# Transformer block on one core: adaLN column sums on VectorE alone, the modulated copy of x on ScalarE, and the residual gate's columns summed in the key projections

## The chip, the cores and the metric

The kernel runs on one core of a Trainium2 chip. The metric is the device time of one execution in microseconds (us), lower is better. The kernel before takes 989.82 us, the median of three runs (989.09 to 990.09).

The names of the engines in the profile: PE is TensorE (matrix products and transposes), DVE is VectorE, ACT is ScalarE, POOL is GpSimd, SP is SyncE, which here issues the transfers. Each engine runs its own instructions strictly in order and waits on semaphores for the others.

## The reference, cut to what matters

One block of a streaming encoder on x of 1024 tokens by 1024 channels, all in float32:

```
shift, scale, gate = split(c @ w_ada + b_ada, 3)
h = rms_norm(x, norm_w) * (1 + scale) + shift
cq, ckv, k_rope, gate_a, q_b, k_b, v_b, f_b, gate_b, mg_a, mg_b = split(h @ w_in)
q  = rms_norm(cq)  @ w_uq          # branch A, 8 heads
kv = rms_norm(ckv) @ w_ukv
o_a = attention_a(norm(q), norm(k), v)        # chunk-causal mask
o_b = attention_b(norm(q_b), norm(k_b), v_b)  # forget gates, causal
merged = sigmoid(mg_a) * ((o_a * silu(gate_a)) @ w_branch_a)
       + sigmoid(mg_b) * ((o_b * silu(gate_b)) @ w_branch_b)
out = x + gate * (merged @ w_out)
```

shift and scale are needed before the first product of h. gate, the residual gate, is needed only in the last line.

## The kernel before, in words

**Precision.** Every product is done in three passes: an operand is split into a high part (a cast to fp32r) and a low part (the rest), and hi·hi, hi·lo and lo·hi are added. So each operand costs a cast, mostly on ScalarE, and a subtraction, mostly on VectorE.

**Order of work.** Nothing schedules the program: each engine's instructions stand in the order in which the Python code emits them. SyncE issues the transfers in the same way, one queue, in order.

**Stage 1** (`phase0`, 0 to about 87 us). x is loaded, normed, transposed and kept as xT, 8 blocks (kt) of 128 channels on the partitions by 1024 tokens. The columns of shift and scale for a block come from two tiles of w_ada (128x1024): each is multiplied by c, spread over all partitions (`cb`), and summed along the row. `ada_cols(kt, e)` does that for tile e (0 is shift, 1 is scale): engine "d" is one VectorE instruction (L339), "p" is the product on GpSimd (L342), and "a" the sum on ScalarE after it (L344). `gain(kt)` makes the factor and the addend of a block, gs (two VectorE instructions, L348 and L349). `high(kt)` writes hT_hi = xT·gs + gs on ScalarE (L355), `modulate(kt)` the same in full precision over xT on VectorE (L359), and `low(kt)` hT_lo = xT - hT_hi on VectorE (L365). Then `products(kt)` adds a block into the q latents: 8 token tiles x 3 passes = 24 matmuls of 424 columns for each block; the last pass reads hT_lo. Blocks 0 and 1 are handled piece by piece as x arrives (token tiles 0 to 5 first, "last" are tiles 6 and 7), blocks 2 to 7 in the loop `for kt in range(2, KT)`, where an iteration makes the gain and the high part of block kt + 1 and the low part of block kt.

**The residual gate before.** In the same loop the 8 tiles of w_gate are loaded (`gate_load`) and summed with c (`gate_sum`): half by GpSimd (L932) and ScalarE (L936), half by VectorE (L939), the last of them in the next stage, `latents`. There the bias is added to the 8 columns, gcol. `gate_row` turns gcol into a row and stores it: a transpose on TensorE (pgT), a scaled copy on VectorE (grow, L949), a transfer to gate_d (L950). It is called in the q projections, after the third pair of token tiles.

**Stage 2** (`g2k`, about 220 to 275 us) is the key and value projection of branch A, two token tiles in each of four calls (sp): kv matmuls, ScalarE copies, the low part of v on VectorE (L831), square sums (L834), rsqrt, the scaled k (L841), and stores to va_d and ka_d one call later (L807). Between and behind the calls `fill_to` puts matmuls that are only due later: here branch B's q, k and v (PSUM tile b, 48 matmuls of 256 columns for each, copied out by ScalarE and VectorE, L883, and stored to vb_d, L918). Two PSUM banks take turns for them. After stage 2 the heads' operands are loaded back (qs from qa_d, L1087, then v, q and ks from ka_d) and the attention starts.

Of the kernel before, what the change touches and what calls it, by code (L numbers as in the profile page):

```python
# [10 lines left out]
F32 = mybir.dt.float32  # L11
# [30 lines left out]
class Slots:  # L42
    """Equal pieces of SBUF, taken and given back by hand; the one given back longest ago goes first."""
# [31 lines left out]
class Net:  # L75
# [162 lines left out]
    # ------------------------------------------------------------ phase 0  # L238
    def phase0(self):
# [46 lines left out]
        def warm(n, src):  # L286
            """Keeps the tensor engine's clock up while it waits for x."""
# [23 lines left out]
        def broadcast_c():  # L311
            """c along the free dimension of every partition, through a diagonal and a product with ones."""
# [15 lines left out]
        def ada_rows(kt, bank):  # L328
            """The shift of a block whose rows lie on the partitions."""
# [6 lines left out]
        def ada_cols(kt, e, engine="d"):  # L336
            w, a = wada[kt][e], acc[:, kt, e:e + 1]
            if engine == "d":
                nc.vector.scalar_tensor_tensor(out=w, in0=w, scalar=1.0, in1=self.cb, op0=ALU.mult, op1=ALU.mult,  # L339
                                               accum_out=a)  # L340
            elif engine == "p":
                nc.gpsimd.tensor_tensor(out=w, in0=w, in1=self.cb, op=ALU.mult)  # L342
            else:
                nc.scalar.activation(w, w, AF.Copy, accum_out=a)  # L344
# [12 lines left out]
        def modulate(kt, sts=range(ST), engine="d"):  # L357
            c = slice(sts[0] * P, (sts[-1] + 1) * P)
            (nc.vector if engine == "d" else nc.gpsimd).tensor_scalar(  # L359
                out=xT[:, kt, c], in0=xT[:, kt, c], scalar1=gs[:, kt, 1:2], scalar2=gs[:, kt, 0:1],  # L360
                op0=ALU.mult, op1=ALU.add)
# [15 lines left out]

        def modulated(kt, sts):
            high(kt, sts)
            modulate(kt, sts)  # L380
            low(kt, sts)
# [67 lines left out]
        ada_cols(2, 0, "p")  # L449
# [3 lines left out]
        high(1, most)  # L453
        banks[4], banks[5] = self.bank("o", "cq_o"), self.bank("f", "cq_f")
        products(0, (4, 5), (0, 1))
        modulate(1, most)
# [7 lines left out]
        ada_cols(2, 0, "a")  # L464
# [4 lines left out]
        load_cq(2)  # L469
        ada_cols(2, 1)  # L470
# [6 lines left out]
        ada_cols(3, 0, "p")  # L477
        load(5)
        for kt in range(2):
            high(kt, last)  # L480
        high(2)
        for kt in range(2):
            modulate(kt, last)
            low(kt, last)
        for kt in range(2):
            products(kt, last)
        ada_cols(4, 0, "p")
        load_cq(3)
        load(6)
        for kt in range(2, KT):  # L490
            if 2 < kt < KT - 2:
                ada_cols(kt + 2, 0, "p")
            if kt + 1 < KT:
                ada_cols(kt + 1, 0, "a")
# [3 lines left out]
            modulate(kt)  # L498
            low(kt)
# [6 lines left out]
            if kt == 5:  # L506
                self.gate_load((0, 1))
                self.gate_sum((0, 1), "p")
            if kt == 6:
                self.gate_load((2, 3))  # L510
                self.gate_sum((0, 1), "a")
                self.gate_sum((2, 3), "p")
            if kt == 7:
                self.gate_load((4, 5))
# [8 lines left out]
    # ------------------------------------------------------------ latents  # L523
# [33 lines left out]
    def latents(self):  # L557
# [43 lines left out]
        self.gate_load((6, 7))  # L601
        self.gate_sum((2,), "a")
        self.gate_sum((4,))
# [7 lines left out]
        self.gate_sum((5, 6, 7))  # L611
# [9 lines left out]
        self.gate_sum((3,), "a")  # L621
# [30 lines left out]
        nc.vector.tensor_tensor(out=self.gcol, in0=self.gcol, in1=self.b_gate, op=ALU.add)  # L652
# [82 lines left out]
    # ------------------------------------------------------------ branch A operands  # L735
# [62 lines left out]
    def store(self, *items):  # L798
        """(dst, src, slot): put on the queue one unit later, when the data is there, so that no load waits behind it.
        A function among them makes more of these when its turn comes."""  # L800
# [44 lines left out]
    # ------------------------------------------------------------ work off the critical path  # L845
    def g1b(self, hook):
        """q, k and v of branch B: 256 columns at a time, two token tiles in a bank."""
# [78 lines left out]
    def gate_sum(self, chs, engine="d"):  # L926
        """128 columns of the adaLN gate each."""
        nc = self.nc
        for ch in chs:
            if engine == "p":  # L930
                w = self.wg[ch]
                nc.gpsimd.tensor_tensor(out=w, in0=w, in1=self.cb, op=ALU.mult)  # L932
                continue
            w = self.wg.pop(ch)
            if engine == "a":
                nc.scalar.activation(w, w, AF.Copy, accum_out=self.gcol[:, ch:ch + 1])  # L936
                self.U.put(w)
                continue
# [4 lines left out]
    def gate_row(self):  # L943
        """The gate as a row, quartered (the two factors of a half that the merge gates leave out)."""
        nc = self.nc
        pg = self.bank("t", "pgT")
# [10 lines left out]
    def fillers(self):  # L957
        """All GEMMs that only have to be done in time, some matmuls at a time; True where an accumulation ends."""
# [172 lines left out]
    def prep_b(self, n):  # L1131
        """The same for heads n and n + 1 of branch B, turned together: rows 0-63 of a transpose are head n's."""
# [16 lines left out]
        def group(nm, src, vec, g):  # L1149
# [41 lines left out]
    def scores(self, n, i):  # L1191
        """Scores of q tile i of head n and their maximum; the rest of the softmax is returned."""
# [35 lines left out]
    def turn(self, n, g, j):  # L1228
        """Transposes k block j of P for q tiles 4g..4g+3; the products with V are returned."""
# [114 lines left out]
    # ------------------------------------------------------------ all  # L1344
# [189 lines left out]
```

## Time and profile before

| | |
|---|---|
| median of three runs | 989.82 us (989.09 to 990.09) |
| profiled execution, span from its first to its last instruction | 989.3 us |
| mean granted clock of TensorE | 0.990 |
| PE busy | 954.5 us, 96% |
| DVE busy | 659.8 us, 67% |
| ACT busy | 475.7 us, 48% |
| POOL busy | 250.8 us, 25% |

The profiled execution has no time of its own in the results; its span is what the trace covers. TensorE is busy nearly everywhere, so the time is the sum of TensorE's work and of the stretches in which it waits. On the page's picture of 40 slices such stretches are in the first four (PE 6, 4, 7, 9 tenths) and in the last one. The granted clock is 1.0 at TensorE's higher level (2.4 GHz) and 0.5 at the lower one (1.2 GHz).

### The profile page before, as it was taken

The numbers are of one execution on the slowest core, as the hardware profiler recorded it, in microseconds if no ns is written. First come the engines' busy times: TensorE is split into PE (matmuls) and PEld (weight loads), VectorE is DVE, ScalarE is ACT, GpSimd is POOL, SyncE is SP. The second block draws the span as 40 slices with busy tenths as digits, with TensorE's granted clock in tenths as the row PEclk, the third lists the DMA queues.
The fourth block names the chain that finished last, engine by engine and source line by source line (L and its number), as shares of the span: only waits on it lengthen the run. The fifth ranks groups of instructions, "written<-read, shape, count | busy, mean of one in ns | idle before, by whom it ended". The sixth has DMA issues, their size and how long they took to land.

```text
span 989.3 us, 15335 instructions
## 1 busy us (share of the span) xinstructions
PE 954.5 (96%) x5550; PEld 833.1 (84%) x5550; DVE 659.8 (67%) x1399; ACT 475.7 (48%) x962; POOL 250.8 (25%) x279
## 2 busy tenths in 40 slices
PE   6479999999999999999999999999999999999998
PEld 6379999999998888888888888888888888887887
DVE  6997787676734766757667667677676767495222
ACT  6347653344334655655646566566565644143000
POOL 4843222220001222221223233333332220045000
PEclk9889999999999999999999999999999999999999
DMA  9733113346485223424224232231321554643321
GB/s 345 285 128 131 52 55 107 124 150 221 155 251 149 67 95 84 139 66 109 84 65 119 77 108 66 86 109 65 118 87 45 181 181 148 228 148 126 100 92 64
DMA packets 80700, 123.95 MB, mean 125 GB/s; under 512 B 5896, under 2 KB 47504, under 8 KB 80624
## 3 DMA queue, kind: packets, MB, share of 16 engines
q1 hardware_dynamic: 80624, 122.96, 38.1%
q8 instruction: 44, 0.72, 0.3%
q14 instruction: 32, 0.26, 0.1%
HBM read 87.29 MB, written 35.66 MB: 124 GB/s over the span
## 4 chain that ended last, share of the span: by engine, by line
PE 85%; DVE 8%; DMA 4%; issue 1%; ACT 1%; SPq 0%; POOL 0%; ACTq 0%; DVEq 0%; POOLq 0%
PE f L127 31%; PE b L127 12%; PE out L127 9%; PE s L127 8%; PE o L127 7%; PE pt L136 6%; PE q L127 3%; PE ckv L127 2%; PE kv L127 2%; DVE hT_lo L1046 1%; DVE hT_lo L365 1%; DMA ks_u<-ka_d 1%; DVE wada_u L339 1%; PE cq_s L127 1%; DVE xT L359 1%
## 5 line engine op out<-in xcount | busy, mean ns | idle before, releaser
L1240 ACT CAST pp_u<-pt 128x512 fp32r<-128x512 f32 x192 | 92.1, 480 | 181.6 <-PE pt L136 167.8
L1241 DVE TENSOR_TENSOR pp_u<-pt,pp_u 128x512 fp32r<-128x512 f32 x192 | 106.6, 556 | 79.2 <-ACT pp_u L1240 77.1
L127 PE MATMUL f<-hT_hi,hi_f_u 128*128 128x512 f32 x384 | 153.6, 400 | 0.0
L127 PE MATMUL f<-hT_hi,lo_f_u 128*128 128x512 f32 x384 | 153.4, 400 | 0.0
L127 PE MATMUL f<-hT_lo,hi_f_u 128*128 128x512 f32 x384 | 153.2, 399 | 0.0
L127 PE MATMUL s<-k_u,q_u 96*128 96x512 f32 (+6 forms) x480 | 116.4, 361 | 0.7 <-ACT p_h L1220 0.7
L127 PE MATMUL b<-hi_b_u,hT_hi 128*128 128x256 f32 x384 | 109.6, 285 | 0.0
L127 PE MATMUL b<-hi_b_u,hT_lo 128*128 128x256 f32 x384 | 108.6, 283 | 0.0
L127 PE MATMUL b<-lo_b_u,hT_hi 128*128 128x256 f32 x384 | 108.6, 283 | 0.0
L1224 POOL TENSOR_SCALAR p_u<-p_u,rs 128x640 f32<-128x640 f32 (+1 forms) x64 | 65.2, 1018 | 164.4 <-DVE rs L1223 95.9
L1224 POOL TENSOR_SCALAR p_h<-p_h,rs 128x128 f32<-128x128 f32 (+1 forms) x64 | 38.6, 603 | 245.5 <-DVE rs L1223 205.7
L1214 DVE TENSOR_REDUCE nm<-s 128x1 f32<-128x128 f32 (+7 forms) x128 | 97.0, 758 | 4.4
L127 PE MATMUL o<-pp_u,v_u 128*128 128x512 f32 (+7 forms) x384 | 94.2, 340 | 0.0
L127 PEld LDWEIGHTS f<-hT_hi,lo_f_u 128*128 128x128 f32 x384 | 72.4, 189 | 11.9
L127 PEld LDWEIGHTS f<-hT_lo,hi_f_u 128*128 128x128 f32 x384 | 72.5, 189 | 11.2
L127 PEld LDWEIGHTS f<-hT_hi,hi_f_u 128*128 128x128 f32 x384 | 72.5, 189 | 11.1
L127 PEld LDWEIGHTS s<-k_u,q_u 96*128 96x128 f32 (+2 forms) x480 | 76.7, 190 | 6.1 <-ACT p_h L1220 1.2
L127 PEld LDWEIGHTS o<-pp_u,v_u 128*128 128x128 f32 (+1 forms) x384 | 61.8, 161 | 19.6
L127 PEld LDWEIGHTS b<-lo_b_u,hT_hi 128*128 128x128 f32 x384 | 73.6, 192 | 0.3
L127 PEld LDWEIGHTS b<-hi_b_u,hT_hi 128*128 128x128 f32 x384 | 73.6, 192 | 0.3
L127 PEld LDWEIGHTS b<-hi_b_u,hT_lo 128*128 128x128 f32 x384 | 73.6, 192 | 0.0
L136 PEld LDWEIGHTS pt<-ident,p_u 128*128 128x128 f32 x416 | 52.7, 140 | 16.6
(319 smaller groups left out, 2072.0 us busy)
## 6 DMA issues: line engine op xcount, KB each, us to landing
raw_f_u<-in_w_t SPq DMA_DIRECT2D x24, 512.0 KB
wada_u<-in_w_ada SPq DMA_DIRECT2D x16, 512.0 KB
mg_d<-th_h SPq DMA_DIRECT2D x32, 256.0 KB
mg_h<-mg_d SPq DMA_DIRECT2D x32, 256.0 KB
raw_b_u<-in_w_b SPq DMA_DIRECT2D x12, 512.0 KB
x_u<-in_x SPq DMA_DIRECT2D x8, 512.0 KB
raw_wg_u<-in_w_gate SPq DMA_DIRECT2D x8, 512.0 KB
va_d<-vhl_u SPq DMA_DIRECT2D x8, 512.0 KB
```

The source lines that it names most:

```text
L127: self.nc.tensor.matmul(out, lhsT=l, rhs=r, start=start, stop=stop)
L136: self.nc.tensor.transpose(out=out, in_=in_, identity=self.ident)
L339: nc.vector.scalar_tensor_tensor(out=w, in0=w, scalar=1.0, in1=self.cb, op0=ALU.mult, op1=ALU.mult, accum_out=a)
L359: (nc.vector if engine == "d" else nc.gpsimd).tensor_scalar(out=xT[:, kt, c], in0=xT[:, kt, c], scalar1=gs[:, kt, 1:2], scalar2=gs[:, kt, ...
L365: nc.vector.tensor_tensor(out=lo[:, kt, c], in0=xT[:, kt, c], in1=hi[:, kt, c].bitcast(F32), op=ALU.subtract)
L1046: nc.vector.tensor_tensor(out=self.hT_lo[x], in0=mA[c1][:, x[2]], in1=self.hT_hi[x].bitcast(F32), op=ALU.subtract)
L1214: nc.vector.tensor_reduce(out=nm, in_=sv, axis=AX.X, op=ALU.max, negate=True)
L1224: nc.gpsimd.tensor_scalar(out=p[:, 0:w], in0=p[:, 0:w], scalar1=rs, scalar2=0.0, op0=ALU.mult, op1=ALU.add)
L1240: nc.scalar.copy(ph[:, c0:], pt[:, c0:])
L1241: nc.vector.tensor_tensor(out=pl[:, c0:], in0=pt[:, c0:], in1=ph[:, c0:].bitcast(F32), op=ALU.subtract)
```

## The change: what is computed where

1. Stage 1: both sums of blocks 2 to 7 are single VectorE instructions. GpSimd's products and ScalarE's sums are gone.
2. Stage 1: `modulate` of block 1 on, and of the last token tiles of block 0, is a ScalarE instruction behind `high` of the same block. In the loop, the low part of block kt now stands first in its iteration.
3. The residual gate's sums leave stage 1 and `latents`. They stand in stage 2: a new input c_row (4 KB) is spread over the partitions by one transfer (cb2, 512 KB in SBUF), two tiles of w_gate are loaded ahead of each of the four calls, and two VectorE sums stand behind each call. `gate_row`, with the bias, follows the fourth.

Other lines of the diff drop comments. `high` is as before (L349 in the changed kernel).

```
     def ada_cols(kt, e):
         w, a = wada[kt][e], acc[:, kt, e:e + 1]
-            elif engine == "p":
-                nc.gpsimd.tensor_tensor(out=w, in0=w, in1=self.cb, op=ALU.mult)
-            else:
-                nc.scalar.activation(w, w, AF.Copy, accum_out=a)
+        nc.vector.scalar_tensor_tensor(out=w, in0=w, scalar=1.0, in1=self.cb,
+            op0=ALU.mult, op1=ALU.mult, accum_out=a)
     def modulate(kt, sts=range(ST), engine="d"):
+        if engine == "a":
+            nc.scalar.activation(xT[:, kt, c], xT[:, kt, c], AF.Identity,
+                scale=gs[:, kt, 1:2], bias=gs[:, kt, 0:1])
+            return
...
         for kt in range(2):
             high(kt, last)
+            modulate(kt, last, "a")
+        for kt in range(2):
+            low(kt, last)
         high(2)
+        modulate(2, engine="a")
         for kt in range(2, KT):
-            if 2 < kt < KT - 2:
-                ada_cols(kt + 2, 0, "p")
+            low(kt)
             if kt + 1 < KT:
-                ada_cols(kt + 1, 0, "a")
+                ada_cols(kt + 1, 0)
                 ada_cols(kt + 1, 1)
                 gain(kt + 1)
                 high(kt + 1)
-            modulate(kt)
-            low(kt)
+                modulate(kt + 1, engine="a")
...
-            if kt == 5:
-                self.gate_load((0, 1))
-                self.gate_sum((0, 1), "p")
...
     def gate_row(self):
+        self.U.put(self.cb)
+        nc.vector.tensor_tensor(out=self.gcol, in0=self.gcol, in1=self.b_gate, op=ALU.add)
         pg = self.bank("t", "pgT")
         self.transpose(pg[0:8, 0:P], self.gcol)
...
                 for sp in range(4):
                     self.g2q(sp)
-                    if sp == 2:
-                        self.gate_row()
...
+                self.cb = self.U.get([P, D], F32, "cb2")
+                nc.sync.dma_start(self.cb, t["c_row"].broadcast_to([P, D]))
+                self.gate_load((0, 1))
                 for sp in range(4):
                     self.g2k(sp)
+                    self.gate_sum((2 * sp, 2 * sp + 1))
+                    if sp < 3:
+                        self.gate_load((2 * sp + 2, 2 * sp + 3))
                     self.fill_to(self.pe_time + 6500)
+                self.gate_row()
                 self.store()
```

VectorE, loop of stage 1, before. A row is the line, the operation and what it writes and reads; wada41 is the scale tile of block 4. These are the iterations for blocks 2 and 3:

```order
L339 SCALAR_TENSOR_TENSOR wada31_u20_21_344,ada_109<-wada31_u20_21_344,cb_u13_14_240 128x1024
L348 TENSOR_SCALAR gs_108<-ada_109,vec_91 128x1
L349 SCALAR_TENSOR_TENSOR gs_108<-ada_109,b1_97,vec_91 128x1
L359 TENSOR_SCALAR xT_107<-xT_107,gs_108 128x1024
L365 TENSOR_TENSOR hT_lo_81<-xT_107,hT_hi_80 128x1024
L339 SCALAR_TENSOR_TENSOR wada41_u3_25_446,ada_109<-wada41_u3_25_446,cb_u13_14_240 128x1024
L348 TENSOR_SCALAR gs_108<-ada_109,vec_91 128x1
L349 SCALAR_TENSOR_TENSOR gs_108<-ada_109,b1_97,vec_91 128x1
L359 TENSOR_SCALAR xT_107<-xT_107,gs_108 128x1024
L365 TENSOR_TENSOR hT_lo_81<-xT_107,hT_hi_80 128x1024
```

The same engine and place in the changed kernel (wada40 is the shift tile of block 4):

```order
L361 TENSOR_TENSOR hT_lo_81<-xT_107,hT_hi_80 128x1024
L338 SCALAR_TENSOR_TENSOR wada30_u19_20_343,ada_109<-wada30_u19_20_343,cb_u13_14_240 128x1024
L338 SCALAR_TENSOR_TENSOR wada31_u20_21_344,ada_109<-wada31_u20_21_344,cb_u13_14_240 128x1024
L342 TENSOR_SCALAR gs_108<-ada_109,vec_91 128x1
L343 SCALAR_TENSOR_TENSOR gs_108<-ada_109,b1_97,vec_91 128x1
L361 TENSOR_TENSOR hT_lo_81<-xT_107,hT_hi_80 128x1024
L338 SCALAR_TENSOR_TENSOR wada40_u2_24_443,ada_109<-wada40_u2_24_443,cb_u13_14_240 128x1024
L338 SCALAR_TENSOR_TENSOR wada41_u3_25_444,ada_109<-wada41_u3_25_444,cb_u13_14_240 128x1024
```

The modulation (L359) has left VectorE, the shift tile's sum has come, and the low part of a block follows the gain of that block directly, with the high part and the modulation on ScalarE between the two.

VectorE at the end of stage 2, before (kraw6 and kraw7 are k of the last two token tiles, bv4_1 and bv4_2 low parts of branch B's v, lo_b5_1 the low part of a weight):

```order
L841 TENSOR_TENSOR kraw6_h3_68_3013<-kraw6_h3_68_3013,y_g2k_3_3079 128x512
L841 TENSOR_TENSOR kraw7_h2_69_3071<-kraw7_h2_69_3071,y_g2k_3_3079 128x512
L883 TENSOR_TENSOR bv4_1_u23_140_3128<-b4_1_3039,bv4_1_u23_140_3128 128x8x64
L116 TENSOR_TENSOR lo_b5_1_u20_142_3133<-raw_b5_1_u19_134_2954,hi_b5_1_u25_141_3132 128x512 x2
L883 TENSOR_TENSOR bv4_2_u11_144_3197<-b4_2_3138,bv4_2_u11_144_3197 128x8x64
```

The same place in the changed kernel (raw_wg6 and raw_wg7 are the last two tiles of w_gate):

```order
L814 TENSOR_TENSOR kraw6_h3_67_2997<-kraw6_h3_67_2997,y_g2k_3_3063 128x512
L814 TENSOR_TENSOR kraw7_h2_68_3055<-kraw7_h2_68_3055,y_g2k_3_3063 128x512
L904 SCALAR_TENSOR_TENSOR raw_wg6_u19_132_2891,gcol_111<-raw_wg6_u19_132_2891,cb2_u28_112_2423 128x1024
L904 SCALAR_TENSOR_TENSOR raw_wg7_u9_133_2893,gcol_111<-raw_wg7_u9_133_2893,cb2_u28_112_2423 128x1024
L856 TENSOR_TENSOR bv4_1_u4_141_3114<-b4_1_3023,bv4_1_u4_141_3114 128x8x64
L116 TENSOR_TENSOR lo_b5_1_u6_143_3119<-raw_b5_1_u20_135_2938,hi_b5_1_u2_142_3118 128x512 x2
L912 TENSOR_TENSOR gcol_111<-gcol_111,vec_91 128x8
L916 TENSOR_SCALAR grow_h4_69_3158<-pgT_3156 8x128
L856 TENSOR_TENSOR bv4_2_u25_145_3189<-b4_2_3124,bv4_2_u25_145_3189 128x8x64
```

Four rows have come in: the two sums, the bias, and the copy of the transposed row; the last two stand behind bv4_1 and a weight's low part.

TensorE around the transpose of gcol, before (it stands in the q projections, behind the transposes of qraw; qrt1 is their PSUM tile):

```order
L136 MATMUL qrt1_2039<-ident_89,qraw2_u19_95_1675 128x128
L136 MATMUL qrt1_2039<-ident_89,qraw3_u20_96_1737 128x128
L136 MATMUL pgT_2049<-ident_89,gcol_111 8x128
L127 MATMUL b1_3_1966<-hi_b1_0_u14_86_1275,hT_hi_80 128x256
L127 MATMUL b1_3_1966<-lo_b1_0_u11_87_1276,hT_hi_80 128x256
```

And in the changed kernel (b4_2 is the third tile of branch B's v, first half):

```order
L127 MATMUL b4_2_3124<-hi_b4_0_u8_122_2608,hT_hi_80 128x256
L127 MATMUL b4_2_3124<-lo_b4_0_u11_123_2609,hT_hi_80 128x256
L127 MATMUL b4_2_3124<-hi_b4_0_u8_122_2608,hT_lo_81 128x256
L136 MATMUL pgT_3156<-ident_89,gcol_111 8x128
L127 MATMUL b4_2_3124<-hi_b4_0_u8_122_2608,hT_hi_80 128x256
L127 MATMUL b4_2_3124<-lo_b4_0_u11_123_2609,hT_hi_80 128x256
L127 MATMUL b4_2_3124<-hi_b4_0_u8_122_2608,hT_lo_81 128x256
```

The transpose has moved from the q projections into the middle of b4_2, 60 b matmuls behind the last kv matmul of stage 2. The transfer to gate_d has moved with it on SyncE's queue: it now stands ahead of the stores va_d and ka_d of token tiles 6 and 7, which `self.store()` behind the loop issues, and of the load qs of the first heads.

## Rows read from the trace of the kernel before

**Rows 1.** Windows: busy us (and count) of PE, PEld, DVE, ACT, POOL, clock, DMA share, GB/s.

```profile
40.00:50.00 10.00, 0.97 (x6) 0.60 (x4) 9.97 (x8) 2.28 (x3) 9.78 (x4) 0.70 0.49 156
50.00:60.00 10.00, 9.89 (x41) 9.50 (x42) 9.90 (x18) 5.46 (x8) 1.73 (x1) 0.78 0.33 108
60.00:70.00 10.00, 6.10 (x32) 5.64 (x31) 9.97 (x6) 2.28 (x3) 9.33 (x4) 1.00 0.60 208
...
71.30:74.80 3.50, 3.50 (x12) 3.29 (x11) 3.47 (x9) 2.96 (x4) 0.00 (x0) 0.51 0.01 2
...
80.00:255.00 175.00, 174.88 (x1373) 171.20 (x1373) 129.38 (x362) 90.36 (x176) 40.11 (x62) 1.00 0.36 119
255.00:275.00 20.00, 20.00 (x148) 19.02 (x147) 16.67 (x45) 6.53 (x12) 0.00 (x0) 1.00 0.66 238
275.00:285.00 10.00, 10.00 (x86) 10.00 (x85) 1.39 (x2) 1.17 (x2) 0.00 (x0) 1.00 1.03 306
```

**Rows 2.** Waits, 18 to 92 us: who waited for whom, total, times, longest.

```profile
ACT hT_hi L355 <- DVE gs L349: 31.2, 8, 5.7
PE cq_t L127 <- DVE hT_lo L365: 9.1, 1, 9.1
```

**Rows 3.** Timeline of DVE, stage 1: start, duration, line, operation, count.

```profile
28.57 2.17 DVE L349 SCALAR_TENSOR_TENSOR gs<-ada,b,vec 128x1 f32<-128x1 f32 x1
...
38.66 3.40 DVE L339 SCALAR_TENSOR_TENSOR wada_u<-wada_u,cb_u 128x1024 f32<-128x1024 f32 x1
...
53.00 1.23 DVE L365 TENSOR_TENSOR hT_lo<-xT,hT_hi 128x1024 fp32r<-128x1024 f32 x1
54.14 1.22 DVE L339 SCALAR_TENSOR_TENSOR wada_u<-wada_u,cb_u 128x1024 f32<-128x1024 f32 x1
...
55.41 0.21 DVE L349 SCALAR_TENSOR_TENSOR gs<-ada,b,vec 128x1 f32<-128x1 f32 x1
55.54 0.81 DVE L359 TENSOR_SCALAR xT<-xT,gs 128x1024 f32<-128x1024 f32 x1
...
67.17 3.24 DVE L365 TENSOR_TENSOR hT_lo<-xT,hT_hi 128x1024 fp32r<-128x1024 f32 x1
```

**Rows 4.** Timeline of ACT, stage 1.

```profile
37.63 1.10 ACT L355 ACTIVATE hT_hi<-xT,gs 128x256 fp32r<-128x256 f32 x2
...
55.72 1.25 ACT L355 ACTIVATE hT_hi<-xT,gs 128x1024 fp32r<-128x1024 f32 x1 [1.17 <-DVE gs L349]
56.87 0.98 ACT L115 CAST hi_cq_u<-raw_cq_u 128x424 fp32r<-128x424 f32 x2
```

**Rows 5.** Timeline of PE, end of stage 1.

```profile
70.46 1.04 PE L127 MATMUL cq_s<-hi_cq_u,hT_lo 128*128 128x424 f32 x4 [4.36 <-DVE hT_lo L365]
...
82.91 0.35 PE L127 MATMUL cq_s<-hi_cq_u,hT_hi 128*128 128x424 f32 x1
...
87.47 0.28 PE L127 MATMUL ckv<-hi_ckv_u,hT_hi 128*128 128x256 f32 x1
```

**Rows 6.** Timeline of DVE, stage 2.

```profile
251.48 0.69 DVE L831 TENSOR_TENSOR vhl_u<-kv,vhl_u 128x512 fp32r<-128x512 f32 x1 [3.57 <-ACT vhl_u L830]
...
267.04 0.69 DVE L831 TENSOR_TENSOR vhl_u<-kv,vhl_u 128x512 fp32r<-128x512 f32 x1 [0.46 <-ACT vhl_u L830]
...
273.24 1.28 DVE L116 TENSOR_TENSOR lo_b_u<-raw_b_u,hi_b_u 128x512 fp32r<-128x512 f32 x2
```

**Rows 7.** Chain that ended last, in order of time: start, us, what (end of stage 2).

```profile
263.15 2.75 PE kv L127 x12
265.89 15.13 PE b L127 x126
...
282.82 10.02 DMA ks_u<-ka_d
...
292.98 0.63 PE kt L136 x4
```

**Rows 8.** Waits, 265 to 340 us.

```profile
PE kt L136 <- DMA ks_u<-ka_d: 1.0, 1, 1.0
```

More of the change, by code (lines that the diff above doesn't have):

```diff
@@ L334, in ada_rows, with ada_cols @@
             return pa[:, 0:1]
-        def ada_cols(kt, e, engine="d"):
+        def ada_cols(kt, e):
             w, a = wada[kt][e], acc[:, kt, e:e + 1]
-            if engine == "d":
-                nc.vector.scalar_tensor_tensor(out=w, in0=w, scalar=1.0, in1=self.cb, op0=ALU.mult, op1=ALU.mult,
-                                               accum_out=a)
-            elif engine == "p":
-                nc.gpsimd.tensor_tensor(out=w, in0=w, in1=self.cb, op=ALU.mult)
-            else:
-                nc.scalar.activation(w, w, AF.Copy, accum_out=a)
+            nc.vector.scalar_tensor_tensor(out=w, in0=w, scalar=1.0, in1=self.cb, op0=ALU.mult, op1=ALU.mult, accum_out=a)
         def gain(kt, a0=None):
@@ L358, in modulate @@
             c = slice(sts[0] * P, (sts[-1] + 1) * P)
-            (nc.vector if engine == "d" else nc.gpsimd).tensor_scalar(
-                out=xT[:, kt, c], in0=xT[:, kt, c], scalar1=gs[:, kt, 1:2], scalar2=gs[:, kt, 0:1],
-                op0=ALU.mult, op1=ALU.add)
+            if engine == "a":
+                nc.scalar.activation(xT[:, kt, c], xT[:, kt, c], AF.Identity, scale=gs[:, kt, 1:2], bias=gs[:, kt, 0:1])
+                return
+            nc.vector.tensor_scalar(out=xT[:, kt, c], in0=xT[:, kt, c], scalar1=gs[:, kt, 1:2], scalar2=gs[:, kt, 0:1],
+                                    op0=ALU.mult, op1=ALU.add)
         def low(kt, sts=range(ST)):
@@ L376, in products @@
                     product(kt, st, e)
[L378 to L381, printed above, removed]
         self.wg = {}
@@ L448, in phase0 @@
         U.put(cqw[0])
-        ada_cols(2, 0, "p")
         ada_cols(1, 1)
@@ L453, in phase0 @@
         high(1, most)
+        modulate(1, most, "a")
         banks[4], banks[5] = self.bank("o", "cq_o"), self.bank("f", "cq_f")
         products(0, (4, 5), (0, 1))
-        modulate(1, most)
         low(1, most)
@@ L463, in phase0 @@
         products(1, most, (2, ))
-        ada_cols(2, 0, "a")
         wh, wl = U.get([P, 2, 424], F32R, "hi_cq1"), U.get([P, 2, 424], F32R, "lo_cq1")
@@ L469, in phase0 @@
         load_cq(2)
+        ada_cols(2, 0)
         ada_cols(2, 1)
@@ L476, in phase0 @@
         banks[6], banks[7] = self.bank("t", "cq_t0"), self.bank("t", "cq_t1")
-        ada_cols(3, 0, "p")
         load(5)
@@ L480, in phase0 @@
             high(kt, last)
+            modulate(kt, last, "a")
+        for kt in range(2):
+            low(kt, last)
         high(2)
-        for kt in range(2):
-            modulate(kt, last)
-            low(kt, last)
+        modulate(2, engine="a")
         for kt in range(2):
             products(kt, last)
-        ada_cols(4, 0, "p")
         load_cq(3)
@@ L505, in phase0 @@
                 self.kvw = [self.load_w(t["w_ckv"][:, 4 * i:4 * i + 4], [P, 4, 256], f"ckv{i}") for i in range(2)]
-            if kt == 5:
-                self.gate_load((0, 1))
-                self.gate_sum((0, 1), "p")
[L509 to L512, printed above, removed]
             if kt == 7:
-                self.gate_load((4, 5))
                 self.kvs = [self.split(w, f"ckv{i}") for i, w in enumerate(self.kvw)]
@@ L599, in kev @@
                 nc.scalar.activation(o[:, i], raw[:, i], AF.Square, accum_out=self.lssq["ckv", st // 4][:, x:x + 1])
-        self.gate_load((6, 7))
-        self.gate_sum((2,), "a")
-        self.gate_sum((4,))
         for st in range(4):
@@ L610, in latents @@
         self.lat_scale(384, 0, "cq")
-        self.gate_sum((5, 6, 7))
         rope = self.rope_tables()
@@ L620, in latents @@
         kev(0)
-        self.gate_sum((3,), "a")
         ckv(2, "s")
@@ L651, in latents @@
         self.lat_scale(256, 1, "ckv")
-        nc.vector.tensor_tensor(out=self.gcol, in0=self.gcol, in1=self.b_gate, op=ALU.add)
         next(rope)
@@ L924, in gate_load, with gate_sum @@
             self.wg[ch] = self.load_w(self.t["w_gate"][ch], [P, D], f"wg{ch}")
-    def gate_sum(self, chs, engine="d"):
+    def gate_sum(self, chs):
         nc = self.nc
         for ch in chs:
[L930 to L933, printed above, removed]
             w = self.wg.pop(ch)
[L935 to L938, printed above, removed]
             nc.vector.scalar_tensor_tensor(out=w, in0=w, scalar=1.0, in1=self.cb, op0=ALU.mult, op1=ALU.mult,
@@ L1380, in build @@
     def build(self):
-        ctx, tc, t = self.ctx, self.tc, self.t
+        ctx, tc, t, nc = self.ctx, self.tc, self.t, self.nc
         dp = ctx.enter_context(tc.tile_pool(name="dr", bufs=1, space=bass.MemoryType.DRAM))
@@ L1491, in layout @@
     o["vec"] = vec
+    o["c_row"] = np.ascontiguousarray(a["c"][0].reshape(1, D))
     o["pos"] = np.ascontiguousarray(a["positions"][0].reshape(8, P).T)
```

## Prediction

> **What bounds the kernel now.** I read the page's engine shares first. TensorE is busy 96% of the span, so a change of the time must come from the places where TensorE waits. The windows show where these are, and the reader is to compare PE with DVE in them. From 40 to 50 us TensorE works 0.97 of 10 us and from 60 to 70 us 6.10, while VectorE is full (9.97) and GpSimd too (9.78, 9.33). From 80 to 255 us and on to 285 us TensorE never stops (174.88 of 175, then 20.00 of 20 and 10.00 of 10) [rows 1]. So stage 1 is bound by VectorE, stage 2 by TensorE. The waits say the same: ScalarE's high part waits 31.2 us in all for the gains, TensorE 9.1 us at once for a low part [rows 2].
>
> The timeline of VectorE tells why it is so slow. The same low part of 1024 columns takes 1.23 us in one place and 3.24 in another, a column sum 1.22 or 3.40, and a gain's one-column instruction 0.21 or 2.17 [rows 3]. The long ones fall in the windows in which GpSimd is full. What lies beside GpSimd's products pays some 2 us each time.
>
> **Stage 1: what the change takes out and puts in.** GpSimd's products and the stretched durations go. I follow the chain that remains.
>
> The gain of block 1 took 2.17 us beside a GpSimd product and will take 0.21 [rows 3]: ScalarE's work behind it, which ends with the copies of x and high(0, last), starts 2.0 us earlier, at 35.7 in place of 37.63 [rows 4]. Then ScalarE has high and modulate of two pieces of 256 columns (1.10 us for two [rows 4], so 2.2 for four) and of block 2. A ScalarE modulation that writes plain float32 is not in the trace. The nearest row is the high part itself, 1.25 us for 1024 columns with the same scale and bias [rows 4]. The casts bound it from below (0.98 us for 848 columns, so 1.18 for 1024), the pieces of 256 columns from above (four of 0.55, 2.2) [rows 4]. I take 1.25, since shape, scale and bias are the same there, and keep both ends. With 0.1 for handing over, low(2) starts at 35.7 + 2.2 + 2.5 + 0.1 = 40.5, against 53.00 [rows 3].
>
> From there VectorE and ScalarE take turns, as the order in the changed kernel shows: low(kt), two sums and the gain on VectorE, then high and modulate on ScalarE, and only then low(kt + 1). From the start of a low part to ScalarE's next high part it was 55.72 - 53.00 = 2.7 us with one sum [rows 3, 4]; with the second sum (1.15, from one start to the next [rows 3]) 3.9. Add high and modulate, 2 x 1.25: 6.4 us for a block. In two of the five turns a cq weight is split too: two casts of 0.98 us together behind the modulation [rows 4] and the last of its two subtractions behind that, and VectorE's low part stands behind both: 7.8. So 3 x 6.4 + 2 x 7.8 = 34.8, low(7) starts at 75.3 and ends at 76.5. TensorE's 24 matmuls for a block take 87.47 - 82.91 = 4.6 us [rows 5], less than a turn, so it follows. Behind low(7) 22 of the last 24 remain, 4.2 us at 0.19, and the ckv products start at 80.7 where they started at 87.47 [rows 5]: 6.8 us earlier.
>
> The clock takes some of it. After a pause of 4.36 us [rows 5] TensorE ran at half its clock from 71.3 to 74.8 us (granted 0.51), which cost 3.5 x 0.49 = 1.7 us; after the one of 9.1 us the 10 us from 50 on were granted 0.78, 2.2 us lost [rows 1]. In the changed kernel each turn has a pause of about 2 us. A drop there is hidden in the turn's own slack (4.6 + 1.7 is 6.3 of 6.4). Only the last counts: a pause of 2.3 us before the first two matmuls of block 7 and of 2.0 behind them, then 22 matmuls. No row has so short a pair of pauses: 0 to 1.7, I take 1.0.
>
> The Trainium skill (TensorE: Matmul & The Clock Gate, "Why this matters for your kernels") warns of idle gaps between bursts of matmuls, since they put the clock back. The rows above agree with it for pauses of 4.36 and 9.1 us. Read as speaking of one unbroken gap it would spare the last turn, and the sum below would come out 1.0 lower; by the nearest row, the pause of 4.36 us, it would come out 0.7 higher.
>
> Stage 1 is worth -6.8 + 1.0 = -5.8. The gate's sums that leave it are off this path: ScalarE and GpSimd had them, and VectorE's own came when TensorE was already full. From 80 us on TensorE is never idle, so the lead carries over to stage 2 unchanged.
>
> **Stage 2: what the gate costs there.** Eight sums come to VectorE, 1.17 us each with their accumulator read, 2.35 us for a call, with GpSimd idle (0.00 [rows 1]). In the first two calls VectorE has gaps such as 3.57 us [rows 6], and nothing is late. In the last two it is full: 16.67 us of 20 [rows 1] and the rest are handovers to ScalarE that don't shrink when VectorE is late, except one of 0.46 us [rows 6]. So VectorE falls 4 x 1.17 - 0.46 = 4.2 us behind. gcol's last addition stands, by the order, behind the weight split that ended at 273.24 + 1.28 = 274.5 [rows 6]; it will be done at 278.9 with 0.2 of its own.
>
> TensorE comes to gcol's transpose earlier. It stands 60 b matmuls behind the last kv matmul, which ended at 265.9; at 15.13 / 126 = 0.12 us each [rows 7] that is 273.1. TensorE takes its instructions in order, so it stands still for 278.9 - 273.1 = 5.8 us with ready b matmuls behind the transpose. In the kernel before nothing waited here. After so long a pause the clock falls as in stage 1: 1.7 us (0 to 2.2).
>
> SyncE is held too: the transfer to gate_d waits for the transposed row and stands ahead of the stores of k and v of the last two tiles and of the load of q. They go out at about 279.5, some 7 us late. Behind them on the queue stand, up to ks of the first head, 5.5 MB; at the 306 GB/s of 275 to 285 us [rows 1] that is 18.0 us, done at 297.5. TensorE, itself 7.5 us late, wants ks at 292.98 - 1.0 + 7.5 = 299.5 [rows 7, 8]. So ks is no longer waited for, and the 1.0 us it cost [rows 8] goes. cb2 and the w_gate tiles add 4.5 MB before that, in a stage whose transfers were busy 0.36 to 0.66 [rows 1]; I price them at nothing.
>
> Stage 2: 5.8 + 1.7 - 1.0 = +6.5.
>
> **The sum.** -5.8 + 6.5 = +0.7 on the profiled span of 989.3, so 990.0. The median of the runs is 0.5 above the span: 990.5. Two large terms cancel, and the unknowns are: ScalarE's modulation (six places on the path; 0.4 less in all at its lower end, 5.7 more at its upper, which is rival C's), the two clock drops (-1.0 to +0.7, -1.7 to +0.5), and handovers between VectorE and ScalarE of up to 0.1 more, twice in five turns (1.0). They don't all fall the same way; the likeliest's own range is 988 to 993.
>
> **Rivals.**
>
> A, TensorE doesn't stand still in stage 2. This needs gcol 5.8 us earlier, or b matmuls that TensorE may do before the transpose. For it: VectorE was only 83% busy from 255 to 275 us [rows 1], and if its 3.3 us of handovers took up the sums, most of the lateness would go. Against it: the order is fixed, and the tile behind the transpose is not the only thing late, since bv4_1 stands behind the sums as well and holds one of the two banks that the b products use. Without any stall 989.3 - 5.8 + 0.5 = 984.0; with the bank's wait, about 2 us, 986.
>
> B, slower: the held transfers become the bound. ks and the operands ahead of it must be there at 299.5. This decides at 5.5 MB in 20 us, 275 GB/s. For it: the same stretch with the row before it averaged (238 x 20 + 306 x 10) / 30 = 261 GB/s [rows 1], and the load of ks took 10.02 us from its issue [rows 7]. Against it: before 275 us the queue was not always full. At 240 GB/s the data is there at 302.4, 2.9 us late; with a second drop of the clock in part (0.6) it gives 990.5 + 3.5 = 994.
>
> C, the turns in stage 1 don't do what they should: VectorE now idles 2.5 us in each turn while ScalarE modulates, work that it did itself in 0.81 [rows 3]. If the modulation costs 1.7, halfway to its upper end, six of them lose 2.7 of the gain: 993.2. For it: two crossings of engines for each block in place of one. Against it: even then no instruction of a turn is as slow as the 3.24 us of a low part beside GpSimd [rows 3].
>
> **How the numbers follow.** A measurement of this kernel can tell a difference of about 0.2%, 2 us, from none; so no change is 987.8 to 991.8. The likeliest case has 0.50, A 0.22, B 0.19, C 0.09. Of the likeliest 0.03 is faster, 0.35 within, 0.12 slower; of A 0.20 is faster and 0.02 within; B is slower; C is 0.06 slower and 0.03 within. Together: faster 0.23, within 0.40, slower 0.37. The range reaches from A's upper part to B's middle, 986 to 994.
>
> **What would show it.** Right: low(2) at about 40 us, turns of 6.4 us with VectorE waiting for ScalarE, ckv at 81 us, then a wait of TensorE for gcol of 5 to 6 us in stage 2 with a lower clock behind it, and no wait for ks. Wrong: no such wait, or one for a bank of b in its place (A); a wait of TensorE for ks or q of the first heads (B); turns of 7 us and more (C). If ckv starts before 78 or after 84 us, the first half failed; if gcol waits less than 3 us, the second.

## The result and the profile after

The changed kernel takes 997.07 us, the median of four runs (995.23 to 998.20), against 989.96 us before (four runs, 989.09 to 990.18). The ratio is 1.0067, 95% interval 1.0053 to 1.0082: 0.7% slower, where 990.5 with a range of 986 to 994 was forecast. The profiled execution took 996.64 us with a span of 994.9, 5.6 us longer than the span of before.

The order of reading is that of the prediction: the turns of stage 1, its head, the stall of stage 2, and what comes behind it. VectorE in the loop of stage 1 of the changed kernel (start, duration, what, and the idle time before it with its releaser):

```profile
43.50 1.23 DVE L361 TENSOR_TENSOR hT_lo<-xT,hT_hi 128x1024 fp32r<-128x1024 f32 x1 [1.99 <-ACT xT L354]
44.64 1.22 DVE L338 SCALAR_TENSOR_TENSOR wada_u<-wada_u,cb_u 128x1024 f32<-128x1024 f32 x1
...
45.78 1.22 DVE L338 SCALAR_TENSOR_TENSOR wada_u<-wada_u,cb_u 128x1024 f32<-128x1024 f32 x1
...
47.05 0.21 DVE L343 SCALAR_TENSOR_TENSOR gs<-ada,b,vec 128x1 f32<-128x1 f32 x1
49.86 1.22 DVE L361 TENSOR_TENSOR hT_lo<-xT,hT_hi 128x1024 fp32r<-128x1024 f32 x1 [2.59 <-ACT xT L354]
```

ScalarE in the same turn:

```profile
47.30 1.24 ACT L349 ACTIVATE hT_hi<-xT,gs 128x1024 fp32r<-128x1024 f32 x1 [3.84 <-DVE gs L343]
48.58 1.25 ACT L354 ACTIVATE xT<-xT,gs 128x1024 f32<-128x1024 f32 x1
```

In the loop no instruction is stretched any more ([rows 3] had 3.40 and 3.24 us for the same work; one column sum ahead of the loop still takes 2.07 us, beside GpSimd's scaling of a token tile). But each engine waits for the other, VectorE 2.59 us and ScalarE 3.84 of the 6.36 us from one low part to the next. From low(2) at 43.50 to low(7) at 78.18 it is 34.7 us, and ckv starts here, where [rows 5] had 87.47:

```profile
83.76 0.28 PE L127 MATMUL ckv<-hi_ckv_u,hT_hi 128*128 128x256 f32 x1
```

That is 3.7 us earlier. Low(2) itself comes 3 us later than forecast. Its reason lies at 20 us, where GpSimd scales two token tiles of x while VectorE makes a column sum and then two square sums (the second row of VectorE here is the first of these two). GpSimd, VectorE and then TensorE of the changed kernel:

```profile
14.66 2.21 POOL L281 TENSOR_SCALAR x_u<-x_u,y_x 128x1024 f32<-128x1024 f32 x2 [1.94 <-ACT xT L309]
18.82 5.15 POOL L281 TENSOR_SCALAR x_u<-x_u,y_x 128x1024 f32<-128x1024 f32 x2 [1.94 <-ACT xT L309]
```

```profile
18.57 1.22 DVE L338 SCALAR_TENSOR_TENSOR wada_u<-wada_u,cb_u 128x1024 f32<-128x1024 f32 x1
...
20.71 1.21 DVE L272 SCALAR_TENSOR_TENSOR junk_h<-x_u 128x1024 bf16<-128x1024 f32 x1
```

```profile
24.02 1.09 PE L136 MATMUL xt<-ident,x_u 128*128 128x128 f32 x8 [2.09 <-POOL x_u L281]
...
25.93 3.51 PE L127 MATMUL pada<-vec,wada_u 128*128 128x64 f32 x16
```

The same pair of scalings takes 2.21 us and then 5.15. TensorE waits 2.09 us for tile 5, and its next 16 small products take 3.51 us, at half the clock (granted 0.50 from 25.9 to 29.5 us; 1.89 us in the kernel before).

Stage 2, waits of TensorE from 255 to 400 us in the changed kernel:

```profile
PE pgT L136 <- DVE gcol L912: 5.7, 1, 5.7
PE kt L136 <- DMA ks_u<-ka_d: 2.9, 1, 2.9
```

and the windows around them, in the columns of [rows 1]:

```profile
270.00:280.00 10.00, 5.02 (x31) 5.03 (x32) 5.79 (x12) 0.59 (x1) 0.00 (x0) 0.66 0.32 127
...
298.00:303.00 5.00, 4.70 (x28) 4.73 (x28) 2.10 (x3) 2.57 (x5) 0.00 (x0) 0.66 0.15 55
```

The first wait is the forecast one. The second is the wait of [rows 8], 1.0 us there: it has not gone, it has grown to 2.9, and behind it the clock falls a second time (granted 0.66). SyncE's issues of this stretch, with what the chain gives for the last of them, in the changed kernel:

```profile
284.09 2.32 SPq L1062 DMA_DIRECT2D q_u<-qr_d  x4
286.59 0.38 SPq L891 DMA_DIRECT2D vb_d<-bv_u  x1
287.30 0.38 SPq L1054 DMA_DIRECT2D ks_u<-ka_d  x1
```

```profile
287.30 10.87 DMA ks_u<-ka_d
```

ks is issued behind the store vb_d of the third b tile, and that store needs the low part that VectorE makes of the tile when TensorE's b matmuls are done. VectorE in the kernel before, then VectorE and TensorE in the changed one:

```profile
281.66 0.69 DVE L883 TENSOR_TENSOR bv_u<-b,bv_u 128x512 fp32r<-128x512 f32 x1 [5.07 <-ACT bv_u L882]
```

```profile
285.17 0.69 DVE L856 TENSOR_TENSOR bv_u<-b,bv_u 128x512 fp32r<-128x512 f32 x1 [5.07 <-ACT bv_u L855]
```

```profile
298.30 0.88 PE L136 MATMUL kt<-ident,ks_u 128*128 128x128 f32 x4 [2.85 <-DMA ks_u<-ka_d]
```

TensorE is ready for the transposes of ks (kt) 9.6 us after this low part, in the kernel before (282.35 to 291.9) as here (285.86 to 295.45). So the earliest issue of ks and the time at which TensorE wants it move together. Before, ks was issued 0.5 us behind the low part, at 282.82, and took 10.02 us [rows 7]. Here it was issued 1.4 us behind it, since SyncE was still busy with the rows of q until 286.41, and took 10.87 us. These two differences, 1.0 and 0.85 us, are what the wait grew by.

### The profile page after: what moved, and what is told of

It is laid out like the page before. It is cut to its first block, busy times and chain, and to the rows that moved or that the text cites. A ratio compares the mean times of both kernels' runs of the same rounds, so it can differ in the third digit from the quotient of the medians.

```text
span 994.9 us, 15313 instructions
## 1 busy us (share of the span) xinstructions
PE 958.5 (96%) x5550; PEld 835.5 (84%) x5550; DVE 646.7 (65%) x1410; ACT 474.9 (48%) x951; POOL 221.0 (22%) x269
## 4 chain that ended last, share of the span: by engine, by line
PE 81%; DVE 7%; DMA 4%; ACT 4%; issue 2%; SPq 1%; POOL 1%; ACTq 0%; DVEq 0%; POOLq 0%
PE f L127 31%; PE b L127 9%; PE out L127 9%; PE s L127 9%; PE o L127 7%; PE pt L136 6%; PE q L127 3%; PE ckv L127 2%; PE kv L127 2%; DVE hT_lo L1013 1%; DVE wada_u L338 1%; DMA ks_u<-ka_d 1%; DMA vb_d<-bv_u 1%; ACT xT L354 1%; DVE mg_h L1006 1%
```

## Experiments

Each "ratio" is the time against the kernel before, measured beside it, with its 95% interval. e1, e5, e6 and e7 leave out the gate's c: its eight sums and their loads are gone, and the other work is the same. They show what the rest costs and are no whole block.

**What stage 1 and stage 2 are worth apart: e1, e5, e2.**

e1 takes the gate out of stage 2.

```
-                    self.gate_sum((2 * sp, 2 * sp + 1))   # and its loads, and cb2
-                self.gate_row()                           # back in g2q, sp == 2
     def gate_row(self):
+        nc.vector.tensor_copy(self.gcol, self.b_gate)     # the bias alone
```

> The changed kernel without the residual gate's sums, their loads and cb2: the transposed row is that of the bias alone, at its old place in the q projections, so the output lacks c in the gate. Theory (stage 1 gained 3.9 us, stage 2 lost all the rest): ckv starts near 83.5 us, no wait of TensorE for gcol, a wait for ks near 1 us as before, and about 986 us, 3 to 5 below the kernel before. Rival (what was lost lies in stage 1 and the attention, stage 2's waits only moved there): 990 or more.

Measured: 995.62 us, ratio 1.0055 (1.0033 to 1.0076). ckv started at 82.53 us, but the edit made a wait of its own:

```profile
PE pgT L136 <- DVE gcol L911: 8.3, 1, 8.3
```

The copy, written where the transpose is, stood behind all that VectorE had queued at that point. The expectation of no wait was a miss, and the run says nothing on the stages. It does show the mechanism of the stall once more, in another stage. e5 puts the copy where before adds the bias:

```
         self.lat_scale(256, 1, "ckv")
+        nc.vector.tensor_copy(self.gcol, self.b_gate)
```

> As e1, the gate's row again of the bias alone, but the bias is copied into gcol in latents, where the kernel before adds it, so that TensorE doesn't wait for it (8.3 us in e1). Theory: ckv near 82 us (83.8 where GpSimd's scaling of x is held up), no wait for gcol, 3 to 6 us below the kernel before, some 986 us. Rival (stage 1 as changed is itself no gain): 990 or more.

Measured: 987.07 us, ratio 0.9954 (0.9936 to 0.9971), ckv at 83.09, no wait for gcol. Without the gate's sums, stage 1 as changed is a gain of 0.5%, and so the gate's part in stage 2 costs more than stage 1 gives. The wait for ks was 2.2 us here, without any gate in stage 2.

e2 does the other half: the kernel before with the gate's sums and row as in the changed kernel, stage 1 untouched otherwise.

```
-            if kt == 5: gate_load, gate_sum "p" ...       # and kt 6, 7, latents
                     self.g2k(sp)
+                    self.gate_sum((2 * sp, 2 * sp + 1))   # loads, cb2, gate_row as changed
```

> The kernel before with only the gate's part of the change. Theory (GpSimd's four gate products stretch VectorE's chain from 58 to 70 us by some 8 us, of which TensorE sees a pause of 4.4 us and a slow clock of 1.7; stage 2 then loses 5.7 for gcol, 1.4 of clock and 1.9 for ks): ckv near 81.5 us, waits as in the changed kernel, about 993 us. Rival (ScalarE's modulation made the whole gain of stage 1, the gate's products cost nothing there): ckv near 87.5 us and 998 to 999 us.

Measured: 994.12 us, ratio 1.0033 (1.0022 to 1.0044); waits of 5.7 us for gcol and 2.1 for ks. And its ckv:

```profile
81.12 0.28 PE L127 MATMUL ckv<-hi_ckv_u,hT_hi 128*128 128x256 f32 x1
```

This is earlier than the changed kernel's 83.76, with VectorE still modulating and with GpSimd's and ScalarE's sums of w_ada still there. So taking the gate's sums out of stage 1 alone gave it at least as much as the whole change did (6.4 us here; 3.7 in the changed kernel's first trace and 6.1 in e12's).

**The turns: e6, e7.** Both are made from e5, so the gate is the bias alone.

e6 has the modulation back on VectorE, in the order of before, without GpSimd's products:

```
                 high(kt + 1)
-                modulate(kt + 1, engine="a")
+            modulate(kt)
+            low(kt)                       # was first in the iteration
```

> e5 with the modulation back on VectorE and in the order of the kernel before; both column sums stay on VectorE, GpSimd and ScalarE's sums stay out (the gate is again the bias alone). Theory (in the changed kernel ScalarE's high and modulate, 2.5 us, stand in each turn while VectorE waits; what helped was taking GpSimd out): a turn takes VectorE 1.14 + 2.3 + 0.35 + 0.82 = 4.6 us in place of 6.36, ckv at 74 to 77 us, 979 to 981 us. Rival 1 (the modulation on ScalarE made the gain): a turn of over 6.4, ckv later than 84, 989 us or more. Rival 2 (loads or TensorE bound the turns): ckv unchanged near 82 us.

e7 keeps it on ScalarE and makes the sums one iteration earlier:

```
             low(kt)
             if kt + 1 < KT:
-                ada_cols(kt + 1, 0)
-                ada_cols(kt + 1, 1)
                 gain(kt + 1)
                 high(kt + 1)
                 modulate(kt + 1, engine="a")
+            if kt + 2 < KT:
+                ada_cols(kt + 2, 0)
+                ada_cols(kt + 2, 1)
```

> e5 with ScalarE's modulation kept, but the two sums of a block one iteration earlier, beside ScalarE's high and modulate of the block before (the gate is again the bias alone). Theory (the turn is a chain across two engines): it shrinks to 2.5 + 1.14 + 0.35 + handovers, 4.2 us, under TensorE's 4.6, so TensorE binds: ckv at 72 to 76 us, 977 to 980 us. Rival (the turn is bound by an engine's own work, or by the loads of w_ada): turns stay above 5.5 us and ckv near 80.

Measured: e6 973.96 us, ratio 0.9831 (0.9813 to 0.9849); e7 972.77, ratio 0.9822 (0.9805 to 0.9839). VectorE in e6, one turn:

```profile
43.59 1.23 DVE L361 TENSOR_TENSOR hT_lo<-xT,hT_hi 128x1024 fp32r<-128x1024 f32 x1
44.73 1.22 DVE L338 SCALAR_TENSOR_TENSOR wada_u<-wada_u,cb_u 128x1024 f32<-128x1024 f32 x1
...
47.28 0.81 DVE L356 TENSOR_SCALAR xT<-xT,gs 128x1024 f32<-128x1024 f32 x1
48.12 1.23 DVE L361 TENSOR_TENSOR hT_lo<-xT,hT_hi 128x1024 fp32r<-128x1024 f32 x1
```

and in e7, two turns apart (the first of them splits a cq weight):

```profile
44.19 1.23 DVE L361 TENSOR_TENSOR hT_lo<-xT,hT_hi 128x1024 fp32r<-128x1024 f32 x1 [0.30 <-ACT xT L354]
...
49.72 1.22 DVE L361 TENSOR_TENSOR hT_lo<-xT,hT_hi 128x1024 fp32r<-128x1024 f32 x1
...
53.79 1.23 DVE L361 TENSOR_TENSOR hT_lo<-xT,hT_hi 128x1024 fp32r<-128x1024 f32 x1 [0.31 <-ACT xT L354]
```

The plain turn falls from 6.36 to 4.53 us in e6 and 4.07 in e7, as expected (4.6 and 4.2). ckv starts at 71.9 and 70.5, some 2 us earlier than expected, and the times lie 5 and 4 us under the expected ranges, since TensorE hardly pauses any more (busy 10.00 of 10 us from 40 to 90 in e7). The rival that the modulation on ScalarE made the gain is refuted: with it on VectorE the kernel is 13 us faster than e5. Rival 2 of e6 and the rival of e7 (the loads, TensorE, or one engine's own work) are out with the shorter turns. What bound the changed kernel's stage 1 was the chain across two engines.

**The stall of stage 2: e3, e4.**

e3 calls the row in the attention:

```
-                self.gate_row()
+        self.extra = [((1, 2), self.gate_row, ())]        # head 1, step 2
```

> The changed kernel with gate_row in the attention (head 1, step 2) in place of behind stage 2; the sums stay. Theory (the wait for gcol goes, but bv4_1's low part stands behind the sums and holds its bank until 273.6 us, where TensorE would come at 271.2): a wait of about 2.4 us for that bank in place of 5.7, the wait for ks still 2 to 3 us since TensorE is earlier by as much as the transfers; about 992 us. Rival 1 (the transpose is the only price): 988 to 989 us. Rival 2 (any late VectorE costs the same, wherever the transpose is): 996 us.

Measured: 992.89 us, ratio 1.0016 (1.0001 to 1.0031). Waits of TensorE from 255 to 400 us in e3:

```profile
PE b L127 <- DVE bv_u L856: 2.3, 1, 2.3
PE pgT L136 <- DVE gcol L911: 1.8, 1, 1.8
...
PE kt L136 <- DMA ks_u<-ka_d: 0.5, 1, 0.5
```

The time and the 2.3 us for the bank are as expected: VectorE's lateness has a second way to TensorE when the transpose is gone. The wait for ks was not (0.5 in place of 2 to 3: issued 0.45 us behind the low part, and there for TensorE 9.6 us later), and a new 1.8 at the transpose's new place was not thought of.

e4 puts the stores ahead:

```
-                self.gate_row()
                 self.store()
+                self.gate_row()
```

> The changed kernel with the stores of k and v of the last two token tiles ahead of the gate's row on SyncE's queue; the wait for gcol stays. Theory (the wait of 2.9 us for ks came from 1.5 MB that was held 5 us behind gate_d): the wait for ks falls under 1 us and the time to about 994.5 us. Rival (ks is late because its own issue stands behind vb_d's last store, whatever was held): the wait stays near 2.9 us and the time near 997.

Measured: 993.93 us, ratio 1.0022 (1.0003 to 1.0041), single runs from 989.2 to 998.1. The time is the theory's, the wait for ks is not: it stayed at 2.2 us. With the stores out of the way SyncE was no longer late, and ks was issued 0.45 us behind the low part in place of 1.4, but its load took 11.2 us. So the held stores cost the issue about 1 us and are not the whole cause; the rival's reason (the place of ks's own issue) holds better, though not its size.

**The wait for ks: e13.**

```
         src = load("q", self.qa_d)
         yield
+        ks = load("k", self.ka_d) if n == 0 else None     # ahead of q's rotary rows
         operands("q")
```

> The changed kernel with the load of ks for the first heads issued ahead of the four loads of q's rotary rows, in place of behind them and behind vb_d's store of the third b tile. Theory (the wait for ks is the 10 to 11 us from its issue to its landing, less the 8 to 9 that TensorE takes from the b tile in front of that store to the transposes of k; it moves with TensorE, so no delay of TensorE takes it away): issue some 4 us earlier, no wait for ks, no low clock behind it, 2 to 4 us below the changed kernel's 994.4, 990 to 992 us; the wait for gcol stays 5.7 us. Rival (all transfers of this stretch land when the whole backlog is through): a wait of 2 us or more stays, at ks or at the rows of q, and the time near 994.

SyncE in e13:

```profile
281.28 0.91 SPq L1054 DMA_DIRECT2D ks_u<-ka_d  x1
282.24 4.52 SPq L1062 DMA_DIRECT2D q_u<-qr_d  x4
286.86 1.29 SPq L891 DMA_DIRECT2D vb_d<-bv_u  x1
```

Its trace has no wait for ks, nor one for the rows of q that now stand behind it, and the clock at 1.00 from 280 to 400 us; the first head's products come 3.3 us earlier than in e12 below (0.1 ahead of the kernel before, where e12 is 3.1 behind), of which 0.5 is from stage 1. So the rival is out: not everything has to wait until the backlog is through, and the place of ks on the queue decides. The median, 993.60 us, ratio 1.0024 (1.0008 to 1.0041), is 0.8 us below e12's, and the intervals overlap: with runs from 990.4 to 996.8, the expected 990 to 992 was missed and the size of the gain stays unclear.

How long the load of ks takes is left open. In the fourteen traces in which it stands behind that store, TensorE was ready 9.6 us after the low part each time, and ks was there for it 9.3 to 11.8 us after its issue: 9.3 in e10 and 11.8 in e11, which differ only in the head of stage 1. The wait was 0.2 to 3.0 us, and 2.2 in e5, where nothing was held and TensorE did not stand still.

**The head of stage 1: e12, e9.** e12 is the changed kernel once more.

> The changed kernel itself once more, beside the kernel before on the same chip. Expected 994 to 998 us with the wait for gcol of 5.7 us and ks of 2 to 3 us again. If GpSimd's second scaling of x lasts 3.1 us in this execution (as in the trace of before and in e1, e5 to e8) low(2) comes at 40 to 41 us, if 5.15 us at 43 to 44.

Measured: 994.40 us, ratio 1.0046 (1.0029 to 1.0062), eight runs of 992.7 to 998.8. In its profiled execution (992.71 us, span 990.9) GpSimd's second scaling was short, VectorE's square sums began behind it, low(2) came at 41.13 us and ckv at 81.38:

```profile
19.54 3.06 POOL L281 TENSOR_SCALAR x_u<-x_u,y_x 128x1024 f32<-128x1024 f32 x2 [1.94 <-ACT xT L309]
```

```profile
23.59 1.21 DVE L272 SCALAR_TENSOR_TENSOR junk_h<-x_u 128x1024 bf16<-128x1024 f32 x1
```

e9 takes tile 5 from GpSimd:

```
-        scale((4, 5), engines="pp")
+        scale((4, 5), engines="pd")
```

> The changed kernel with x's token tile 5 scaled by VectorE in place of GpSimd (one word). Theory (in the changed kernel's trace GpSimd's second scaling, 3.0 of 5.15 us, lay beside VectorE's square sums and was held up; TensorE waited 2.1 us for tile 5 and ran the next 7 us at the lower clock; low(2) came at 43.5 in place of 40.5 us): no wait of TensorE for a tile of GpSimd after 20 us, low(2) near 41 us, and 1 to 3 us below the changed kernel of the same call. Rival (the 3 us come from the clock alone, whoever scales tile 5): low(2) stays at 43 to 44 us, the same time as the changed kernel.

Measured: 993.30 us, ratio 1.0029 (1.0019 to 1.0039); low(2) at 40.08. The median is 1.1 us under e12's, with intervals that overlap; but the spans of its eight runs lie within 2.1 us (990.7 to 992.8) where e12's lie within 6.1 (990.9 to 997.0). That fits the hold-up as the source of the changed kernel's spread, but does not show it. Only profiled executions show which of them had it: the long scaling stands in those of the changed kernel, e2, e3 and e4, where the clock was 1.00 from 10 to 20 us, and not in before, e1, e5 to e8, e10 or e12 to e14, where it was 0.83 to 0.91. It was 0.83 in e9's too, so the low(2) of that execution does not test the edit.

**Versions that beat both: e8, e10, e11, e14.** e8 is e7 with the whole gate on VectorE in latents (sums 0 to 2 at its start, 3 to 5 behind the first scale, 6 and 7 behind the first ckv squares), c as it lies there, no new input.

> e7 with the whole gate: its eight sums on VectorE in latents, where the kernel before had four, with c as it lies there (no new input), the bias in latents and the row in the q projections as before. Theory (VectorE has 5 us free before its first rsqrt and more behind): at most 1 us over e7, 977 to 981 us, and no wait for gcol or more than 1 us for ks. Rival (eight sums delay the latents' rsqrt and turns, so TensorE waits there): 4 us or more over e7, with waits for cqT or ckvT between 90 and 150 us.

Measured: 976.26 us, ratio 0.9853 (0.9832 to 0.9874), 3.5 over e7 where at most 1 was expected, with a new wait of TensorE of 1.9 us for cqT's low part at 85 us. e10 moves the last two sums behind the rope tables:

```
         kev(0)
-        self.gate_sum((6, 7))
...
         next(rope)
+        self.gate_sum((6, 7))
         kev(2)
```

> e8 with the last two of the gate's sums behind the rope tables' second part in place of behind the first ckv squares. Theory (in e8 these two stood ahead of cqT's low part and cost TensorE 1.9 us): no wait for cqT's low part, 973 to 975 us, 1 to 2 below e8. Rival (VectorE then delays the second half's rsqrt): a wait of TensorE between 95 and 105 us and no gain.

Measured: 975.26 us, ratio 0.9851 (0.9833 to 0.9870). That wait is gone and another of 1.8 us has come at 100 us, for the scaled ckv rows, as the rival had it: no clear difference from e8. e11 is e10 with e9's edit:

> e10 with tile 5 of x on VectorE as in e9, a candidate for the best. If GpSimd's hold-up of tile 5 costs 1 to 3 us in some executions, the median falls 0.5 to 2 us below e10 and the spread shrinks; if not, the same as e10.

Measured: 977.29 us, ratio 0.9864 (0.9848 to 0.9880): no gain, with a wait for ks of 2.6 us in its trace, so it doesn't bear out that the hold-up costs 1 to 3 us. e14 is e10 with e13's edit:

> e10 with the same earlier load of ks. Theory: e10's trace waited only 0.2 us for ks, but e11's 2.6, so the median falls by 0 to 2 us: 973 to 975 us. Rival: 0.5 or more over e10, if the rows of q come late.

Measured: 974.64 us, ratio 0.9834 (0.9813 to 0.9856), four runs of 973.6 to 975.7, and no wait for ks. It is the fastest that computes the whole block, 16 us under the kernel before; from e8 and e10 it can't be told apart.

## Why the prediction was wrong, step by step

The likeliest case had two large terms of opposite sign. Both mechanisms were there, and their sum missed.

**The turns: right.** 6.36 and 7.81 us were measured for 6.4 and 7.8, five of them 34.7 for 34.8. Rival C (dearer modulation) is out: ScalarE's modulation took 1.25 us. But the row that mattered more was beside the path: that VectorE waits 2.6 us in each turn was priced as no loss, and e6 and e7 show that 10 us of gain lay there.

**The head, "starts 2.0 us earlier, at 35.7": wrong in the profiled execution, right in others.** ScalarE came to high(0, last) at 38.67 us, since tile 5 of x was late; in e12, the same kernel, at 36.32, in e1 and e13 at 35.8 to 35.9. The prediction took one execution's order between GpSimd and VectorE for the kernel's. The clock's part at the end of stage 1 (0 to 1.7, 1.0 taken) came out at either end: from low(7) to ckv it took 5.6 us in the changed kernel and e12 (next to nothing lost) and 7.15 in e5 (1.6 more). In all, stage 1 gave 3.7 us in place of 5.8, and 6.1 in e12.

**The stall: right.** 5.74 us for 5.8. The 14 matmuls behind it at 0.21 us each in place of 0.12 cost 1.3 for 1.7. Rival A is out.

**"So ks is no longer waited for, and the 1.0 us it cost goes": the step that failed.** It reckoned when the backlog would be through, 297.5 us, and set that against a TensorE that had been delayed. But ks's own load was not in the queue by then. It is issued behind a store that TensorE's b tile releases, and TensorE wants it 9.6 us after VectorE's low part of that tile, so a delay of TensorE delays the earliest issue by as much and leaves the load no more time. From the transfer to gate_d to the landing of ks it took 22.5 us (275.70 to 298.17) where 18.0 were reckoned. The wait was 2.85 us, 1.8 more than before in place of 1.0 less, and the clock fell behind it, some 1.5 us more that no term had. That is 4.4 us of the miss. Rival B had the place, the sign and the size (2.9 us late) right, and its reason in part: what was held made ks's issue about 1 us late here. But the same wait came with nothing held (2.2 us in e5), with the stores ahead (2.2 in e4), and went with the place on the queue alone (e13). How much of the 1.8 us belongs to the change and how much to the load's own time, which varies, stays open.

**The base.** The prediction took the runs to be 0.5 us above the span. In every run with a listed span the time is 1.7 to 2.2 us above it. So the profiled execution of before was one of about 991 us, slower than the four runs of the result (989.09 to 990.18), and the forecast added 1.3 us too little to the span. On the other side, that execution lost 1.3 us near 895 us (granted clock 0.87 from 890 to 900 us), which the changed kernel's did not (1.00). In the forecast of the time the two about cancel.

Matmul by matmul against the trace of before, the changed kernel is 3.8 us ahead in stage 2, 3.5 behind after the stall, 6.9 behind after the wait for ks, and 5.6 at the end. Added up for the profiled span: 0.7 forecast, + 2.0 for stage 1, - 0.2 for the stall and its clock, + 4.4 for ks, - 1.3 at the end gives the 5.6 that were measured.

**Open** is also how much of the difference between 997.07 and e12's 994.40 is the share of executions with the long scaling: only traced executions show it, and the intervals of the two ratios overlap.

## What to carry to other kernels

When work moves from one engine to another, follow the chain of a loop turn through both: a step that nothing disturbs any more still lengthens the turn if the two engines then take turns waiting, and making the independent part (here the sums) one iteration earlier took that away (4.07 us in place of 6.36). A load that is issued behind work of the engine that waits for it moves with that engine: a delay of that engine does not hide the wait, and here an earlier place on the queue did. And before two large terms are set against each other, look at how far single runs of the same kernel spread.

## What the runs showed of the hardware

GpSimd's scaling of two tiles took 2.2 us undisturbed, 3.1 beside one column sum of VectorE, and 5.15 beside that sum and two square sums, in executions of one and the same program (e12 and the changed kernel). In the trace of before TensorE's clock had fallen just ahead of it (granted 0.84 from 10 to 20 us), VectorE came to its square sums at 22.0 us and GpSimd was through; in the changed kernel the clock was 1.00 there, VectorE came at 20.7, and GpSimd was still at work. All four traces with the long scaling have 1.00 in that stretch, the other twelve 0.83 to 0.91. So a lower clock early was followed by a better course later. And a wait of TensorE of 2.2 us left the clock at 1.00 in e12 and was followed by 0.50 for 3 us in e5.
